# Transposes of the second token pair moved between the first products, two gate tiles for HGRN's output, and a modulation chunk moved to the last phase

## The chip, the cores and the metric

The kernel runs on one core of one Trainium2 chip. The metric is the device time of one execution in microseconds (us); several runs are summarised by their median. The profile is of one such execution.

## The reference, cut to what matters

The reference is a two-layer backbone on 512 latent tokens (and 256 context tokens) of width 1024. Each layer is half a SwiGLU feed-forward, a token mixer, and half a feed-forward; each of these is modulated before and normalised after:

```python
def modulation(cond, w_mod, b_mod):
    m = jax.nn.silu(cond) @ w_mod + b_mod          # 9 rows of 1024 a layer ("chunks")
def modulate(x, m, k):
    return x * (1 + m[..., 3 * k + 1, :]) + m[..., 3 * k, :]
def post_norm_update(x, y, m, k, g, b):
    return layer_norm(DN_ALPHA * x + m[..., 3 * k + 2, :] * y, g, b)
...
    for i in range(DEPTH):
        x = macaron_half_ffn(x, mx, 0, ffn_w_in[i, 0], ffn_w_out[i, 0], ln_g[i, 0], ln_b[i, 0])
        ...                                         # mixer: HGRN2 in layer 0, chunk-MLP in layer 1
        x = post_norm_update(x, yx, mx, 1, ln_g[i, 1], ln_b[i, 1])
        x = macaron_half_ffn(x, mx, 2, ffn_w_in[i, 1], ffn_w_out[i, 1], ln_g[i, 2], ln_b[i, 2])
```

All is float32.

## The kernel before

**Products.** Each float32 operand is split into a high and a low part: ACT copies the high part (L135), DVE subtracts it to get the low part (L136), and three matmuls (L148, L149, L150) make one product. The tiles `w` (weights), `xm` (the modulated input), `hs` (hidden units) and `f` (sums of blocks of `xm`) hold such pairs. SP loads the raw weights (`raw`, `rawu`).

**Phases.** The program is a row of output phases (class `OutPhase`, method `run`), each followed by the first products of the next block (classes `FeedIn`, `FeedSums`, `GateIn` and the like, called `nxt`). An output phase multiplies the hidden units by the second weight matrix for four tiles of 128 tokens (`nt`; two in a context phase) and two halves of 512 output columns. `lead` does this pair by pair of hidden blocks. When a half is done, `evac` multiplies each tile's sum `y` by the gate row (`rgate`, L356) and adds the residual (L358), with statistics behind (L361); after the second half `norm` finishes them (L366, two steps on POOL, L380).

**Hand-over.** Then `operand(p, kb)` makes the next input for a pair `p` of token tiles and a pair `kb` of feature blocks: four transposes on PE into `pt` (L390), the modulation by scale and shift (L400 on ACT, L402 on DVE), and the split into `xm`. There are eight such steps, o0 to o3 for tiles 0 and 1, o4 to o7 for tiles 2 and 3. `nxt.staged(p, kb)` multiplies the same piece by the first four weight units (24 matmuls for a feed-forward phase: s0 to s7). In the phases called f2 (after HGRN's output), f3 (after the first layer's last feed-forward), gin (before the chunk-MLP) and f4 (after the chunk-MLP's output) the flag `hold` is set, and two pairs of the output product of the last tile are held back and done between the steps.

**Sums.** FeedSums multiplies 2 by 2 blocks with seven products (`seven`) instead of eight: f2, f3 and f4 first add blocks of the input (`sums`, L601), and the first `seven` (`early`) interleaves these sums with its weight sums. The products are `psc`, `pse`, `psa`, `psb`; the staged ones are `psf`.

**Modulation rows.** The rows of `modulation` are computed on DVE beside other work: `scraps(pool, layer, chunks)` queues them and `mod_step(n)` does n steps for each pair of `lead`; one step loads 512 KB of the modulation weights and does two multiply-and-sum rows on DVE (L170). Chunk 8 of layer 1 is the gate of the very last feed-forward.

**Order.** Each engine has its own in-order queue. A scheduler (the tile framework) places the instructions of each engine; the order written in `run` and the number of buffers of a tile (`bufs`) decide what it can place where.

Of the kernel before, what the change touches and what calls it, by code (L numbers as in the profile page):

```python
# [28 lines left out]
NH = 8  # L29
# [41 lines left out]
def backbone_kernel(  # L71
# [148 lines left out]
    def scraps(sp, l, chs, small=None):  # L220

        if small is None:
            s, small = (sp.tile([P, D], F32, tag="e", name="e", bufs=2) for _ in range(2))
        else:
            s, small = small[:, :D], small[:, D:]
        nc.sync.dma_start(s, cond[CI_OF["x"]].partition_broadcast(P))
        nc.scalar.activation(s, s, AF.Silu)
        small = Scraps(sp, small, "rawu")
        for ch in chs:
            queue_mod(small, {"x": s}, l, ch, ["x"])  # L230

    def queue_mod(modp, srow, l, ch, conds):
        mod_queue.append(mod_task(modp, srow, l, ch, conds))
# [3 lines left out]
    def mod_step(n, after=None):  # L237

        credit[0] += n
        while credit[0] >= 1 and mod_queue:  # L240
            try:
                with tc.issue_after((after or latest[0]).ins):
                    next(mod_queue[0])
                credit[0] -= 1
            except StopIteration:
                mod_queue.pop(0)
        if not mod_queue:
            credit[0] = 0.0

    def made(key):  # L250
        d = gate_row if key[1] % 3 == 2 else mod_col
        while key not in d:
            mod_step(1 - credit[0])
        return d[key]
# [15 lines left out]
    def load_row(pool, tag, src, n=HC, bufs=1):  # L270
        r = pool.tile([P, n], F32, tag=tag, name=tag, bufs=bufs)
        nc.sync.dma_start(r, src.partition_broadcast(P))
        return r

    class OutPhase:
# [49 lines left out]

        def load_gate(self, hf):
            c = slice(hf * HC, (hf + 1) * HC)
            self.gate = load_row(self.bp, "rgate", made((self.l, 3 * self.j + 2, self.cond))[0, c])

        def store(self):  # L330

# [50 lines left out]
        def operand(self, p, kb):  # L382

            o, ks = slice(p * 2 * P, (p + 1) * 2 * P), slice(2 * kb, 2 * kb + 2)
            cols, xm = self.cols, self.xm
            pt = bank("pt").rearrange("p (k t) -> p k t", t=2 * P)
            for i in range(2):
                k = 2 * kb + i
                for t in range(2):
                    nc.tensor.transpose(  # L390
                        pt[:, i, t * P : (t + 1) * P], self.xs[2 * p + t][:, k * P : (k + 1) * P], ident
                    )
            xf = self.nxt.block(p, kb)
            if xf is None:
                xf = pt
            for i in range(2):
                k = 2 * kb + i
                g, b = cols[:, 0, k : k + 1], cols[:, 1, k : k + 1]
                if i or p or kb:
                    nc.scalar.activation(xf[:, i, :], pt[:, i, :], AF.Identity, scale=g, bias=b)  # L400
                else:
                    nc.vector.tensor_scalar(xf[:, i, :], pt[:, i, :], g, b, ALU.mult, ALU.add)  # L402
            return split(xm[:, 0, ks, o], xm[:, 1, ks, o], xf)

        def run(self, bp, hook=None, nmod=0):
            self.bp, nt, nxt = bp, self.nt, self.nxt
            self.xs, self.st = [], []
            self.load_gate(0)
            for t in range(nt):
                xt = bp.tile([P, D], F32, tag="x", name="x", bufs=NT)  # L410
                nc.sync.dma_start(xt, self.xsrc(t))
                self.xs.append(xt)
                self.st.append(bp.tile([P, 2, 6], F32, tag="st", name="st", bufs=NT))
            if self.affine:
                self.lead(0, 3, nmod)
                self.finish()
            self.lead(0, self.npair, nmod)
            for t in range(nt):
                self.evac(0, t)
            if hook:  # L420
                hook()
            self.load_gate(1)
            self.lead(1, self.npair - self.tail, nmod)
            held = [(kk, *self.operands(1, kk)) for kk in range(self.npair - self.tail, self.npair)]
            if nxt is None:
                self.last = [load_row(wpool, "raw", src[self.l, self.j], D, 3) for src in (ln_g, ln_b)]
            else:
                self.cols = operand_cols(self.l, self.j, *self.after, self.cond)
                nxt.load()

            back = 2 if nxt is not None and nxt.hold else 0
            rest = [(1, *h, [nt - 1]) for h in held[len(held) - back :]]
            for t in range(nt):
                for h in held[: len(held) - back * (t == nt - 1)]:
                    self.part(1, *h, [t])

            def done(p):
                for t in (2 * p, 2 * p + 1):
                    self.evac(1, t)
                    self.norm(t)  # L440

            def close():
                self.held.close()
                if self.release:
                    self.release()

            if nxt is None:
                close()
                done(0)
                done(1)  # L450
                return
            nxt.ahead(0)
            done(0)
            steps = [(p, kb) for p in range(nt // 2) for kb in range(KD // 2)]
            for i in range(len(steps) + 3):
                if i == back:
                    for r in rest:
                        self.part(*r)
                    close()
                    nxt.enter()  # L460
                    if nt > 2:
                        done(1)
                if i:
                    nxt.ahead(i)

                if back and i == 4:
                    nxt.staged(*steps[1])
                    nxt.staged(*steps[2])
                if i < len(steps):
                    self.operand(*steps[i])  # L470
                j = i - 2 if back and i > 3 else i - 3
                if 0 <= j < len(steps) and not (back and i == 4):
                    nxt.staged(*steps[j])
            nxt.sums()
            if self.xdst is not None:
                if nxt.whole:
                    nxt.later = self.store()
                else:
                    for t, z in enumerate(self.xs):
                        nc.sync.dma_start(self.xdst(t), z)  # L480
# [546 lines left out]
    with sbuf(name="hgo", bufs=1) as hgo, ExitStack() as late:  # L1027
# [4 lines left out]
        with sbuf(name="hg", bufs=1) as hg:  # L1032
# [226 lines left out]
            def gated(h, on, g):  # L1259
# [8 lines left out]
            op = OutPhase(  # L1268
                lambda k: hts[k], NH, lambda hf, kk: hg_w_out[hf, kk], NT, 0, 1, "x", 1.0,
                lambda t: x1[t], True, (0, 2), None, lambda t: x2[t], f2, tail=3,  # L1270
            )
            prev, done, last = None, None, None
            for h in range(NH + 1):
# [27 lines left out]
                if prev:  # L1301
                    on = outputs(h - 1, prev)
                    g, last = proj_silu(h - 1, 3, "g")
                    done = (h - 1, on, g)
# [13 lines left out]
    with sbuf(name="sp2", bufs=1) as sp, sbuf(name="hp2", bufs=1) as hp, bpools() as bp:  # L1318
# [6 lines left out]
        op = OutPhase(  # L1325
            hget, NF, ffn_units(0, 1), NT, 0, 2, "x", 0.5, lambda t: x2[t], True, (1, 0),
            xm, lambda t: x3[t], f3, tail=3,
        )
# [7 lines left out]
        op = OutPhase(  # L1336
            hget, NF, ffn_units(1, 0), NT, 1, 0, "x", 0.5, lambda t: x3[t], True, (1, 1),
            xm, lambda t: x4[t], gin, tail=3,
        )
# [5 lines left out]
    with ExitStack() as vhp_stack:  # L1345
# [3 lines left out]
        op = OutPhase(  # L1349
            lambda k: hs[k // 3][:, k % 3, :], CI // P, lambda hf, kk: cm_w_out[hf, kk], NT, 1, 1, "x", 1.0,  # L1350
            lambda t: x4[t], True, (1, 2), None, lambda t: x5[t], f4, tail=3,
        )
        op.affine = (1, 0)
        with sbuf(name="cm", bufs=1) as cm, ExitStack() as late:
# [30 lines left out]
            cu, sp = (late.enter_context(sbuf(name=n, bufs=1)) for n in ("cu", "csp"))  # L1385
# [60 lines left out]
            for j in range(0, 3 * NG, 2):  # L1446
# [8 lines left out]
                if j == 3 * NG - 2:  # L1455
                    gin.place.close()
                    mods = ExitStack()
                    modp = mods.enter_context(swap("modp4"))
# [6 lines left out]
        f4.xm = op.xm = xm  # L1465
        bp, bw = (vhp_stack.enter_context(x) for x in (bpools(), sbuf(name="bw4", bufs=1)))
        small = vhp.tile([P, NT, GC], F32, tag="vh", name="vt").rearrange("p t c -> p (t c)")
        scraps(modp, 1, (7, 6, 8), small)
        op.run(bp, None, 1.5)

    with sbuf(name="sp4", bufs=1) as sp, sbuf(name="hp4", bufs=1) as hp, bpools() as bp:
        hget = f4.rest(hp, sp)
        op = OutPhase(
            hget, NF, ffn_units(1, 1), NT, 1, 2, "x", 0.5, lambda t: x5[t], True, None,
            None, lambda t: out[t], None, tail=4,
        )
        op.affine = (1, 1)
        op.run(bp)

# [75 lines left out]
```

## Time and profile before

| what | value |
|---|---|
| runs | 2481.15, 2485.2, 2486.4 us; median 2485.2 |
| profiled execution | 2486.62 us, span 2484.9 us |
| granted TensorE clock, mean | 0.994 |
| PE busy | 2428.3 us (98%), 14907 matmuls |
| DVE busy | 1944.7 us (78%) |
| ACT busy | 1166.0 us (47%) |
| moved by DMA | 365.49 MB, mean 147 GB/s |

The span is the profiled time from the first to the last instruction; the device time includes a little around it. PE is nearly always busy, so its idle stretches and the stretches in which its clock was lowered are what can be shortened. The places that the change touches, in microseconds from the start of the span: HGRN's output ends and f2 begins at 960 to 1060; f3 at 1318 to 1420; gin at 1690 to 1800; the chunk-MLP's output at 2012 to 2120 and f4 to 2200; the last output phase at 2320 to the end.

### The profile page before, as it was taken

The numbers are of one execution on the slowest core, as the hardware profiler recorded it, in microseconds if no ns is written. First come the engines' busy times: TensorE is split into PE (matmuls) and PEld (weight loads), VectorE is DVE, ScalarE is ACT, GpSimd is POOL, SyncE is SP. The second block draws the span as 40 slices with busy tenths as digits, with TensorE's granted clock in tenths as the row PEclk, the third lists the DMA queues.
The fourth block names the chain that finished last, engine by engine and source line by source line (L and its number), as shares of the span: only waits on it lengthen the run. The fifth ranks groups of instructions, "written<-read, shape, count | busy, mean of one in ns | idle before, by whom it ended". The sixth has DMA issues, their size and how long they took to land.

```text
span 2484.9 us, 38142 instructions
## 1 busy us (share of the span) xinstructions
PE 2428.3 (98%) x14907; PEld 2194.3 (88%) x14907; DVE 1944.7 (78%) x3466; ACT 1166.0 (47%) x1821; POOL 43.4 (2%) x83
## 2 busy tenths in 40 slices
PE   7999999999999999999999999999999999899998
PEld 5888889987888888999988899889999987899986
DVE  7965678685588886788895988897898687788775
ACT  4222345454445452555543555544654442555641
POOL 0000000000000000000000000000000000000001
PEclk9999999999999999999999999999999999999999
DMA  8866556783211214333473233574323376333332
GB/s 317 294 204 199 174 187 219 261 252 125 68 60 52 60 60 154 101 116 102 153 247 126 87 110 110 177 238 139 98 100 102 111 248 201 119 116 103 102 117 74
DMA packets 106853, 365.49 MB, mean 147 GB/s; under 512 B 12408, under 2 KB 13616, under 8 KB 106672
## 3 DMA queue, kind: packets, MB, share of 16 engines
q1 hardware_dynamic: 106672, 363.06, 44.3%
q8 instruction: 116, 1.90, 0.3%
q14 instruction: 65, 0.53, 0.1%
HBM read 350.40 MB, written 12.61 MB: 146 GB/s over the span
## 4 chain that ended last, share of the span: by engine, by line
PE 78%; DVE 13%; ACT 3%; DMA 3%; issue 2%; POOL 1%; SPq 0%; POOLq 0%; DVEq 0%; ACTq 0%
PE y L150 7%; PE y L149 7%; PE y L148 7%; PE psf L150 6%; PE psf L149 6%; PE psf L148 6%; PE psc L148 5%; PE psc L150 5%; PE psc L149 5%; PE pse L148 3%; PE pse L150 3%; PE pse L149 3%; DVE w L136 2%; PE psa L149 1%; PE psa L148 1%
## 5 line engine op out<-in xcount | busy, mean ns | idle before, releaser
L136 DVE TENSOR_TENSOR w<-raw,w 128x1024 fp32r<-128x1024 f32 (+2 forms) x446 | 501.0, 1127 | 156.4 <-ACT w L135 155.4
L135 ACT ACTIVATE w<-raw 128x1024 fp32r<-128x1024 f32 (+2 forms) x446 | 436.4, 982 | 388.5 <-PE y L150 89.8
L150 PE MATMUL y<-w,hs 128*128 128x512 f32 x984 | 385.2, 392 | 8.2 <-DVE hs L136 8.2
L148 PE MATMUL y<-w,hs 128*128 128x512 f32 x984 | 385.1, 391 | 0.1
L149 PE MATMUL y<-w,hs 128*128 128x512 f32 x984 | 384.1, 390 | 0.0
L150 PEld LDWEIGHTS y<-w,hs 128*128 128x128 f32 x984 | 185.4, 189 | 49.3 <-DVE hs L136 10.9
L135 ACT ACTIVATE hs<-h 128x512 fp32r<-128x512 f32 (+1 forms) x220 | 125.9, 588 | 201.6 <-PE y L150 186.8
L148 PEld LDWEIGHTS y<-w,hs 128*128 128x128 f32 x984 | 185.3, 188 | 39.3 <-ACT hs L135 0.8
L149 PEld LDWEIGHTS y<-w,hs 128*128 128x128 f32 x984 | 185.5, 189 | 38.3
L148 PE MATMUL psf<-xm,w 128*128 128x512 f32 (+1 forms) x544 | 192.8, 358 | 13.0 <-ACT xm L135 12.8
L150 PE MATMUL psf<-xm,w 128*128 128x512 f32 (+1 forms) x544 | 192.3, 354 | 2.4 <-DVE w L136 2.4
L149 PE MATMUL psf<-xm,w 128*128 128x512 f32 (+1 forms) x544 | 192.6, 354 | 1.5 <-DVE xm L136 1.5
L136 DVE TENSOR_TENSOR hs<-h,hs 128x512 fp32r<-128x512 f32 (+1 forms) x220 | 135.2, 634 | 73.3 <-ACT hs L135 73.1
L148 PE MATMUL pse<-f,w 128*128 128x256 f32 x544 | 155.8, 286 | 5.0 <-ACT w L135 4.1
L148 PE MATMUL psc<-f,w 128*128 128x256 f32 x544 | 156.0, 287 | 4.6 <-ACT w L135 3.8
L150 PE MATMUL pse<-f,w 128*128 128x256 f32 x544 | 155.4, 286 | 0.0
L150 PE MATMUL psc<-f,w 128*128 128x256 f32 x544 | 155.4, 286 | 0.0
L149 PE MATMUL pse<-f,w 128*128 128x256 f32 x544 | 155.2, 285 | 0.0
L149 PE MATMUL psc<-f,w 128*128 128x256 f32 x544 | 154.9, 285 | 0.0
L150 PE MATMUL psc<-xm,w 128*128 128x256 f32 x532 | 151.3, 284 | 2.8 <-DVE w L136 2.8
L148 PE MATMUL psc<-xm,w 128*128 128x256 f32 x532 | 152.1, 286 | 1.8 <-ACT w L135 1.2
L149 PE MATMUL psc<-xm,w 128*128 128x256 f32 x532 | 151.0, 284 | 0.0
(343 smaller groups left out, 6028.7 us busy)
## 6 DMA issues: line engine op xcount, KB each, us to landing
raw<-in_ffn_w_in SPq DMA_DIRECT2D x160, 512.0 KB, 4.5
raw<-in_ffn_w_out SPq DMA_DIRECT2D x110, 512.0 KB, 4.2
mraw<-in_mod_w SPq DMA_DIRECT2D x80, 512.0 KB, 4.5
rawu<-in_mod_w SPq DMA_DIRECT2D x64, 512.0 KB, 4.4
rawu<-in_ffn_w_in SPq DMA_DIRECT2D x60, 512.0 KB, 3.6
x<-x SPq DMA_DIRECT2D x36, 512.0 KB, 3.6
raw<-in_hg_wf SPq DMA_DIRECT2D x32, 512.0 KB, 3.5
raw<-in_cm_w_out SPq DMA_DIRECT2D x24, 512.0 KB, 4.6
```

Of the source, the lines that this page charges most:

```text
L135: nc.scalar.activation(dst_hi, src, AF.Copy)
L136: latest[0] = nc.vector.tensor_tensor(dst_lo, src, dst_hi.bitcast(F32), ALU.subtract)
L148: nc.tensor.matmul(ps, ah, bh, start=start, stop=False, **kw)
L149: nc.tensor.matmul(ps, ah, bl, start=False, stop=False, **kw)
L150: return nc.tensor.matmul(ps, al, bh, start=False, stop=stop, **kw)
```

## The change

Four edits: `run` has a new order for phases with `hold` (written out as a list of o and s), `operand` gives the modulation of the first of its two feature blocks to DVE in every step, `load_gate(0)` comes before the last two pairs of the first half with two gate tiles in HGRN's output alone, and chunk 8 is queued in the last phase instead of the chunk-MLP's output.

```diff
--- before.py
+++ after.py
@@ -325,7 +325,8 @@
 
         def load_gate(self, hf):
             c = slice(hf * HC, (hf + 1) * HC)
-            self.gate = load_row(self.bp, "rgate", made((self.l, 3 * self.j + 2, self.cond))[0, c])
+            row = made((self.l, 3 * self.j + 2, self.cond))[0, c]
+            self.gate = load_row(self.bp, "rgate", row, bufs=2 if self.nk == NH else 1)
 
         def store(self):
 
@@ -396,7 +397,7 @@
             for i in range(2):
                 k = 2 * kb + i
                 g, b = cols[:, 0, k : k + 1], cols[:, 1, k : k + 1]
-                if i or p or kb:
+                if i:
                     nc.scalar.activation(xf[:, i, :], pt[:, i, :], AF.Identity, scale=g, bias=b)
                 else:
                     nc.vector.tensor_scalar(xf[:, i, :], pt[:, i, :], g, b, ALU.mult, ALU.add)
@@ -405,7 +406,6 @@
         def run(self, bp, hook=None, nmod=0):
             self.bp, nt, nxt = bp, self.nt, self.nxt
             self.xs, self.st = [], []
-            self.load_gate(0)
             for t in range(nt):
                 xt = bp.tile([P, D], F32, tag="x", name="x", bufs=NT)
                 nc.sync.dma_start(xt, self.xsrc(t))
@@ -414,6 +414,8 @@
             if self.affine:
                 self.lead(0, 3, nmod)
                 self.finish()
+            self.lead(0, self.npair - 2, nmod)
+            self.load_gate(0)
             self.lead(0, self.npair, nmod)
             for t in range(nt):
                 self.evac(0, t)
@@ -452,25 +454,29 @@
             nxt.ahead(0)
             done(0)
             steps = [(p, kb) for p in range(nt // 2) for kb in range(KD // 2)]
-            for i in range(len(steps) + 3):
-                if i == back:
-                    for r in rest:
-                        self.part(*r)
-                    close()
-                    nxt.enter()
-                    if nt > 2:
+            if not nxt.hold:
+                close()
+                nxt.enter()
+                for i in range(len(steps) + 3):
+                    if i == 1 and nt > 2:
                         done(1)
-                if i:
-                    nxt.ahead(i)
-
-                if back and i == 4:
-                    nxt.staged(*steps[1])
-                    nxt.staged(*steps[2])
-                if i < len(steps):
+                    if i:
+                        nxt.ahead(i)
+                    if i < len(steps):
+                        self.operand(*steps[i])
+                    if i >= 3:
+                        nxt.staged(*steps[i - 3])
+            else:
+
+                for i in range(2):
                     self.operand(*steps[i])
-                j = i - 2 if back and i > 3 else i - 3
-                if 0 <= j < len(steps) and not (back and i == 4):
-                    nxt.staged(*steps[j])
+                for r in rest:
+                    self.part(*r)
+                close()
+                nxt.enter()
+                done(1)
+                for kind, i in ("o2", "o3", "s0", "s1", "o4", "o5", "s2", "o6", "o7", "s3", "s4", "s5", "s6", "s7"):
+                    (self.operand if kind == "o" else nxt.staged)(*steps[int(i)])
             nxt.sums()
             if self.xdst is not None:
                 if nxt.whole:
@@ -1465,8 +1471,8 @@
         f4.xm = op.xm = xm
         bp, bw = (vhp_stack.enter_context(x) for x in (bpools(), sbuf(name="bw4", bufs=1)))
         small = vhp.tile([P, NT, GC], F32, tag="vh", name="vt").rearrange("p t c -> p (t c)")
-        scraps(modp, 1, (7, 6, 8), small)
-        op.run(bp, None, 1.5)
+        scraps(modp, 1, (7, 6), small)
+        op.run(bp, None, 1)
 
     with sbuf(name="sp4", bufs=1) as sp, sbuf(name="hp4", bufs=1) as hp, bpools() as bp:
         hget = f4.rest(hp, sp)
@@ -1475,7 +1481,8 @@
             None, lambda t: out[t], None, tail=4,
         )
         op.affine = (1, 1)
-        op.run(bp)
+        scraps(sp, 1, (8,))
+        op.run(bp, None, 1)
```

Lines of the changed kernel are shifted: L356 is L357 there, L402 is L403, L601 is L607, L661 is L667.

DVE's queue at f3's hand-over before, from the last tile's second-half evacuation (`st` are its statistics, `mv` mean and variance) to the first sums (L601):

```order
1378 L361 BN_STATS st<-x 128x6
1379 L136 TENSOR_TENSOR xm<-h,xm 128x2x256
1380 L366 BN_AGGR mv<-st 128x2
1381 L136 TENSOR_TENSOR xm<-h,xm 128x2x256
1382 L380 TENSOR_SCALAR x<-x,mv,rstd 128x1024
1383 L136 TENSOR_TENSOR xm<-h,xm 128x2x256 x4
1384 L136 TENSOR_TENSOR w<-raw,w 128x1024
1385 L601 TENSOR_TENSOR h<-h 128x512 x4
1386 L680 TENSOR_TENSOR e<-raw,rawu 128x512
1387 L136 TENSOR_TENSOR f_12769<-h,f_12769 128x512 x2
```

The same place in the changed kernel; L403 is the modulation:

```order
1387 L362 BN_STATS st<-x 128x6
1388 L403 TENSOR_SCALAR h<-pt,opc 128x256
1389 L367 BN_AGGR mv<-st 128x2
1390 L136 TENSOR_TENSOR xm<-h,xm 128x2x256
1391 L381 TENSOR_SCALAR x<-x,mv,rstd 128x1024
1392 L136 TENSOR_TENSOR xm<-h,xm 128x2x256
1393 L403 TENSOR_SCALAR h<-pt,opc 128x256 x2
1394 L136 TENSOR_TENSOR xm<-h,xm 128x2x256 x2
1395 L403 TENSOR_SCALAR h<-pt,opc 128x256 x2
1396 L136 TENSOR_TENSOR xm<-h,xm 128x2x256 x2
1397 L136 TENSOR_TENSOR w<-raw,w 128x1024
1398 L607 TENSOR_TENSOR h<-h 128x512 x4
```

Before, the second pair's modulations were all on ACT and have no row here; now each of its steps has one modulation on DVE, ahead of its `xm` split. On PE the transposes of o4 and o5 stood behind s0, s1 and s2, and those of o6 and o7 behind s3 and s4; now o4 and o5 stand behind s1, and o6 and o7 behind s2.

SP's queue at the end of HGRN's output before: loads of the gate rows (`rgate`), the residual (`x`), the next weights and the affine rows (`rg`, `rb`):

```order
202 L141 DMA raw<-in_ffn_w_in 128x1024 x4
203 L272 DMA rgate<-gr_5_x 128x512
204 L411 DMA x<-x_83 128x1024 x4
205 L661 DMA raw<-in_ffn_w_in 128x1024
206 L272 DMA rgate<-gr_8_x 128x512
207 L272 DMA rg<-in_ln_g 128x512
208 L661 DMA raw<-in_ffn_w_in 128x1024
209 L272 DMA rgate<-gr_5_x 128x512
210 L272 DMA rb<-in_ln_b 128x512
```

The same place in the changed kernel:

```order
200 L141 DMA raw<-in_ffn_w_in 128x1024 x4
201 L411 DMA x<-x_83 128x1024 x4
202 L272 DMA rgate<-gr_5_x 128x512 x2
203 L667 DMA raw<-in_ffn_w_in 128x1024 x2
204 L669 DMA rawu<-in_ffn_w_in 128x1024
205 L486 DMA x_84<-x 128x1024
206 L669 DMA rawu<-in_ffn_w_in 128x1024
```

Both halves of the gate row are loaded together, behind the four x loads; the next phase's gate row and the affine rows have gone from between them to later rows.

DVE's queue in the chunk-MLP's output before, from within the evacuation of the third tile's first half to the next split of hidden units (`hs`); `vt` is the modulation's scratch:

```order
2182 L358 TENSOR_TENSOR x<-x,t_19822 128x512
2183 L170 SCALAR_TENSOR_TENSOR vt<-rawu,vt 128x512
2184 L361 BN_STATS st<-x 128x6
2185 L356 SCALAR_TENSOR_TENSOR t_19826<-y_19265,rgate 128x512
2186 L170 SCALAR_TENSOR_TENSOR vt<-rawu,vt 128x512
2187 L358 TENSOR_TENSOR x<-x,t_19826 128x512
2188 L170 SCALAR_TENSOR_TENSOR vt<-rawu,vt 128x512
2189 L361 BN_STATS st<-x 128x6
2190 L183 TENSOR_REDUCE vt<-vt 128x8
2191 L170 SCALAR_TENSOR_TENSOR vt<-rawu,vt 128x512
2192 L194 SCALAR_TENSOR_TENSOR mc_6_x<-vt,mbT 128x8
2193 L136 TENSOR_TENSOR hs<-ht,hs 128x512
```

The changed kernel, from the evacuation of the second tile on:

```order
2194 L136 TENSOR_TENSOR w<-raw,w 128x1024
2195 L362 BN_STATS st<-x 128x6
2196 L357 SCALAR_TENSOR_TENSOR t_19798<-y_19263,rgate 128x512
2197 L136 TENSOR_TENSOR hs<-ht,hs 128x512
2198 L359 TENSOR_TENSOR x<-x,t_19798 128x512
2199 L136 TENSOR_TENSOR hs<-ht,hs 128x512
2200 L362 BN_STATS st<-x 128x6
2201 L357 SCALAR_TENSOR_TENSOR t_19802<-y_19264,rgate 128x512
2202 L170 SCALAR_TENSOR_TENSOR vt<-rawu,vt 128x512
2203 L359 TENSOR_TENSOR x<-x,t_19802 128x512
2204 L170 SCALAR_TENSOR_TENSOR vt<-rawu,vt 128x512
2205 L362 BN_STATS st<-x 128x6
```

The next `hs` splits stand two tiles earlier, and there are fewer modulation rows between the evacuations.

## Prediction

> **What bounds the kernel.** I read the page first, then the windows stage by stage, then the timelines of PE and DVE where PE stands. The page:
>
> ```profile
> PE 2428.3 (98%) x14907; PEld 2194.3 (88%) x14907; DVE 1944.7 (78%) x3466; ACT 1166.0 (47%) x1821; POOL 43.4 (2%) x83
> PE 78%; DVE 13%; ACT 3%; DMA 3%; issue 2%; POOL 1%; SPq 0%; POOLq 0%; DVEq 0%; ACTq 0%
> ```
>
> PE is the bound: it idles 2484.9 − 2428.3 = 56.6 us in all, and DVE carries 13% of the chain of waits. The change removes no matmul, so it can only win idle time of PE, and time at a lowered clock. The windows say where that lies (length, then busy us of PE, PEld, DVE, ACT, POOL, then PEclk, the granted clock, and the DMA share):
>
> ```profile
> 960.00:1010.00 50.00, 46.37 (x290) 41.44 (x289) 29.00 (x45) 16.01 (x27) 3.78 (x8) 1.00 0.62 216
> 1010.00:1060.00 50.00, 47.71 (x369) 46.02 (x368) 48.01 (x73) 31.56 (x54) 0.00 (x0) 0.97 0.26 85
> 1318.00:1372.00 54.00, 53.53 (x352) 48.94 (x351) 31.03 (x48) 22.01 (x39) 3.49 (x8) 1.00 0.36 123
> 1372.00:1420.00 48.00, 42.16 (x320) 40.97 (x319) 43.77 (x66) 26.68 (x46) 0.00 (x0) 0.93 0.32 99
> 1690.00:1800.00 110.00, 109.61 (x624) 106.19 (x623) 93.79 (x136) 65.28 (x109) 3.48 (x8) 1.00 0.35 119
> 2012.00:2070.00 58.00, 51.40 (x214) 41.63 (x213) 53.84 (x120) 18.76 (x26) 0.00 (x0) 0.94 0.70 222
> 2147.00:2200.00 53.00, 47.10 (x360) 45.91 (x359) 48.27 (x71) 29.55 (x50) 0.00 (x0) 0.94 0.47 154
> 1376.78:1380.19 3.41, 2.93 (x12) 2.63 (x12) 3.41 (x6) 0.59 (x2) 0.00 (x0) 0.50 0.16 23
> ```
>
> Idle plus (1 − PEclk) × length gives what each stage can win at most: end of HGRN's output 3.6; f2's first seven products 2.3 + 1.5 = 3.8; f3 0.5 + 5.8 + 3.4 = 9.7; gin 0.4; chunk-MLP output 6.6 + 3.5 = 10.1; f4 5.9 + 3.2 = 9.1. Together 36.7 us. The last row is one of the half-clock stretches: 3.41 us at 0.50, so 1.7 us lost each.
>
> **f3 (run's new order, modulation split).** PE's timeline, and DVE's behind it:
>
> ```profile
> 1353.81 1.03 PE L390 MATMUL pt<-ident,x 128*128 128x128 f32 x8
> 1357.55 0.60 PE L390 MATMUL pt<-ident,x 128*128 128x128 f32 x4
> 1360.86 0.60 PE L390 MATMUL pt<-ident,x 128*128 128x128 f32 x4
> 1376.25 0.39 PE L148 MATMUL psc<-f,w 128*128 128x256 f32 x1 [1.85 <-ACT w L135]
> 1386.21 0.39 PE L150 MATMUL psc<-xm,w 128*128 128x256 f32 x1 [1.42 <-DVE w L136]
> 1389.70 0.39 PE L148 MATMUL pse<-f,w 128*128 128x256 f32 x1 [2.04 <-ACT w L135]
> ```
>
> ```profile
> 1349.82 0.81 DVE L380 TENSOR_SCALAR x<-x,mv,rstd 128x1024 f32<-128x1024 f32 x1 [0.77 <-POOL rstd L370]
> 1356.47 0.69 DVE L136 TENSOR_TENSOR xm<-h,xm 128x512 fp32r<-128x512 f32 x1 [5.84 <-ACT xm L135]
> 1357.59 0.69 DVE L136 TENSOR_TENSOR xm<-h,xm 128x512 fp32r<-128x512 f32 x1 [0.43 <-ACT xm L135]
> 1359.90 0.69 DVE L136 TENSOR_TENSOR xm<-h,xm 128x512 fp32r<-128x512 f32 x1 [1.61 <-ACT xm L135]
> 1363.22 0.69 DVE L136 TENSOR_TENSOR xm<-h,xm 128x512 fp32r<-128x512 f32 x1 [2.63 <-ACT xm L135]
> 1364.96 1.29 DVE L601 TENSOR_TENSOR h<-h 128x512 f32<-128x512 f32 x2
> ```
>
> The waits named "w" are the end of a longer story. DVE idles 5.84 + 0.43 + 1.61 + 2.63 = 10.5 us between 1350 and 1363, because the second pair's transposes (8, 4 and 4) come between blocks of staged products; the last four stand at 1360.86. Only then can the block sums (L601) start, at 1364.96, 3.5 us after those transposes end at 1361.46; from there DVE is full and PE waits for it.
>
> In the new order o4 and o5 follow two blocks instead of three, o6 and o7 one block later. A block is 24 matmuls; that from the first of these transposes to the next is 1357.55 − 1353.81 = 3.74 us, less eight transposes (1.03, with the last one's overlap off 0.87), so 2.9. Tile 3 is normalised at 1350.6, about when the second block ends (2.9 before 1353.81), so o4 waits 0 to 0.4 us for DVE there. Then 0.9 for o4 and o5, 2.9 for a block, 0.9 for o6 and o7: transposes done about 1355.3. With the same 3.5 us behind them the sums start about 1358.8, 6.2 us earlier.
>
> What the earlier start buys: the three quoted waits and two of 0.28 and 0.26 between them make 5.85, and the first half-clock stretch holds PE back another 1.7, so DVE is about 7.5 us late at the last wait. Less 6.2 leaves 1.3. Gain 9.7 − 1.3 − 0.4 = 8.0. Ends: 9.7 if nothing remains; 3 if the start moves by half as much.
>
> The price of the split stands in these rows:
>
> ```profile
> L402 DVE TENSOR_SCALAR h<-pt,opc x2: 529/529/529, 1340.9 to 1699.9; 128x256 f32<-128x256 f32 x2
> L400 ACT ACTIVATE h<-pt,opc x30: 549/565/589, 1341.1 to 1717.8; 128x256 f32<-128x256 f32 x30
> L170 DVE SCALAR_TENSOR_TENSOR vt<-rawu,vt x48: 671/684/695, 1992.9 to 2085.8; 128x512 bf16<-128x512 f32 x48
> ```
>
> Seven modulations a phase go to DVE at 0.53 us (some 0.45 start to start), 3.2 us a phase, 38 in all or 17 us. In f2, f3 and f4 they fall into the idle 10.5 us, so they cost nothing; without that cover the 3.2 would stand ahead of the sums. ACT gets 38 × 0.565 = 21 us back, but it is 47% busy and that is worth nothing.
>
> **f4 and f2.** f4 has the same order and shape; gain by the same steps 9.1 − 1.3 = 7.8 (ends 3 and 9.1). f2 has idle of the same size before its sums and loses 3.8 behind them, less than the sums gain: 3.6 (ends 1.5 and 3.8).
>
> **gin.** Its blocks hold half as many matmuls, so two of them cover less of the normalisation of tile 3 than in f3; the idle there, 0.4, may go and a new wait may come. I take 0 (ends −0.4, and +1.5, twice the 0.77 for which the quoted normalisation waits).
>
> **HGRN's output end (two gate tiles).**
>
> ```profile
> 959.71 0.43 SPq L272 DMA_DIRECT2D rgate<-gr_x  x1
> 965.41 0.69 DVE L356 SCALAR_TENSOR_TENSOR t<-y,rgate 128x512 f32<-128x512 f32 x1 [5.50 <-DMA rgate<-gr_x]
> 978.42 0.69 DVE L356 SCALAR_TENSOR_TENSOR t<-y,rgate 128x512 f32<-128x512 f32 x1 [2.71 <-DMA rgate<-gr_x]
> 983.53 0.44 PE L390 MATMUL pt<-ident,x 128*128 128x128 f32 x2 [1.40 <-DVE x L380]
> 986.19 0.88 PE L390 MATMUL pt<-ident,x 128*128 128x128 f32 x6 [2.23 <-DVE x L380]
> 962.00:966.00 4.00, 4.00 (x19) 3.32 (x18) 0.59 (x1) 1.06 (x1) 0.00 (x0) 1.00 0.76 270
> 966.00:970.00 4.00, 4.00 (x20) 3.30 (x19) 3.90 (x7) 1.06 (x1) 0.00 (x0) 1.00 1.01 391
> ```
>
> Before, gate 0 is the first load and gate 1 waits for the tile. Now both are issued at once, but behind four x loads of 512 KB on SP's queue, 2.1 MB. Of that up to 0.8 landed before the gate anyway (4 us at 270 GB/s, less the gate's 0.26 MB); the other 1.3 at 391 GB/s put gate 0 3.2 us later, at 968.6. DVE does two weight splits (1.13 each) in that wait instead of behind it, and gate 1's 2.71 is gone, so that the second half's evacuation starts 3.2 − 2.3 − 2.7 = 1.8 us earlier, at 976.6. Gain 1.7. Ends: 3.6 (both PE waits go) and a loss of 1.5 (gate 0 two us later still, up to which 978.42 would be kept, and more beyond).
>
> **Chunk-MLP output (a chunk fewer).**
>
> ```profile
> 2043.65 0.68 DVE L356 SCALAR_TENSOR_TENSOR t<-y,rgate 128x512 f32<-128x512 f32 x1
> 2059.44 0.69 DVE L136 TENSOR_TENSOR hs<-ht,hs 128x512 fp32r<-128x512 f32 x1
> 2060.18 0.79 PE L150 MATMUL y<-w,hs 128*128 128x512 f32 x1 [5.21 <-DVE hs L136]
> ```
>
> From 2043.65 the first half's evacuation and ten modulation rows (0.61 start to start, two to a step) stand ahead of the hs split at 2059.44, for which PE waits 5.21. With one step a pair instead of 1.5 DVE's order brings the next hs split into the second tile's evacuation, with one modulation row ahead of it. That wait goes, and the half clock behind it: 5.2 + 3.5 = 8.7; I take 8.0, for 0.7 that the gate row, now ahead of a row of the affine part on SP's queue, can add to the 1.4 us that remain early in the stage. Ends 9 and 0.
>
> **Last phase (chunk 8 added).** Eight steps, that is 16 rows or 10 us of DVE, and their eight loads of 512 KB on SP's queue move here; SP also passes the gate's store and load:
>
> ```profile
> 1240.00:1310.00 70.00, 70.00 (x311) 57.96 (x310) 62.95 (x120) 29.31 (x40) 0.00 (x0) 1.00 0.70 231
> 2320.00:2410.00 90.00, 90.00 (x538) 80.63 (x538) 64.86 (x89) 47.28 (x74) 0.00 (x0) 1.00 0.37 115
> ```
>
> DVE has 25 of 90 us free there, and the first row is an output phase that carries one step a pair already, with PE full at DMA share 0.70. The gate is now made and read back in the phase that uses it; DVE may wait 3 us for it at the first evacuation, with hs splits done 3 pairs ahead. So 0 (ends 0 and +2).
>
> **The phase before the context's output.** Here the split has no cover:
>
> ```profile
> 395.00:405.00 10.00, 9.99 (x84) 9.75 (x83) 9.90 (x19) 10.00 (x20) 0.00 (x0) 1.00 0.71 233
> 397.98 1.22 DVE L136 TENSOR_TENSOR w<-raw,w 128x1024 fp32r<-128x1024 f32 x1
> 406.98 0.28 PE L148 MATMUL psf<-xmc,w 128*128 128x256 f32 x1
> ```
>
> DVE is 99% busy and gets seven modulations or 3.2 us more, and DVE's order puts the weight split of 397.98 behind all operands, some 6 us later. PE wants it at 406.9, it was there at 399.1: the margin of 7.8 shrinks to about 1.8 and holds. 0 (ends 0 and +3).
>
> **Sum:** −8.0 − 7.8 − 3.6 − 1.7 − 8.0 = −29.1 us. The profiled execution took 2486.6, 1.4 over the median of the runs shown; so 2457.5 by the profile, 2456 as a median.
>
> **The clock.** In this trace each half-clock stretch of 3.41 us follows a wait of PE of 1.2 to 5.2 us (1376.78 follows that of 1.85). [...]
>
> **Rivals.**
> - *DVE stays the bound.* The sums start 3 us earlier, not 6.2, because the new DVE rows and the weight splits line up ahead of them. For it: DVE is full from 1365 on. Against it: 10.5 us of idle. f3, f4 gain 3 to 3.5 each, f2 2: −6.5 − 2 − 1.7 − 8 = −18, 2467.
> - *The half clock stays*, because it has another cause than these waits: 3.4 + 3.2 + 1.5 + 3.5 = 11.6 of the gain is not had, 2468. The order of wait and stretch in the rows speaks against it. [...]
> - *Slower: DVE's queue, not the transposes, sets when the sums start.* Then every moved modulation stands on the path, 38 × 0.45 = 17, against 9.7 from the gate tiles and the chunk: 2485 + 7 = 2492. It decides if f3's sums start no earlier than 1364.96. The idle rows speak against it.
> - *The last phase pays for its chunk:* 5 us of waits at the first half's end as in the stage the chunk left: 2461.
> - *No change:* the waits are for weights that come late for another reason (DMA): 2485. DMA shares of 0.26 to 0.47 in those windows speak against it.
>
> **Chances.** Forecast 0.62 (own range 2450 to 2463), DVE stays the bound 0.19, half clock stays 0.05, last phase pays 0.04: faster by over 0.2% (5 us, about what a measurement tells from no change) 0.90. No change 0.04, slower 0.06. The range 2446 to 2470 takes in the full 36.7 below, and the first two rivals above.
>
> **What would show it.** Right: at f3 16 transposes done by 1356, sums near 1359, PE idle from there to 1420 under 2 us; PEclk 1.00 in that window; no 5-us wait in the chunk-MLP output; one wait for a gate at HGRN's output, near 968. Wrong: sums in f3 later than 1362, a PE wait near 407 in the context's phase, or PE waiting for hs near the last phase's first evacuation.

## The result, and the profile after

The changed kernel takes 2453.03 us (median; 2452.43 to 2453.68), the kernel before 2485.07 (2481.15 to 2486.4): a ratio of 0.9874, 95% interval 0.9857 to 0.9891. That is 32 us faster; 2456 was forecast, in a range of 2446 to 2470. The profiled execution has a span of 2452.0 us, 32.9 less than before. Its page, by which PE idles 2452.0 − 2415.9 = 36.1 us instead of 56.6:

```profile
PE 2415.9 (99%) x14907; PEld 2185.4 (89%) x14907; DVE 1959.3 (80%) x3504; ACT 1151.4 (47%) x1784; POOL 44.3 (2%) x83
```

PE busy also fell by 12.4 us, with the same 14907 matmuls: that is the half clock gone (the granted clock was 0.994 before and is 0.999 now, which over the two spans makes 14.9 and 2.5 us lost). The windows that answer to those of before, moved with the program (length; busy us of PE, PEld, DVE, ACT, POOL; granted clock, DMA share, GB/s):

```profile
960.00:1010.00 50.00, 46.38 (x289) 40.97 (x288) 37.28 (x61) 15.71 (x25) 3.78 (x8) 1.00 0.43 156
1010.00:1060.00 50.00, 49.49 (x411) 49.08 (x410) 49.01 (x74) 31.94 (x54) 0.00 (x0) 1.00 0.48 164
1310.00:1364.00 54.00, 53.88 (x344) 48.81 (x343) 39.18 (x62) 21.85 (x36) 3.45 (x8) 1.00 0.38 128
1364.00:1412.00 48.00, 47.92 (x396) 47.42 (x395) 47.01 (x69) 29.69 (x51) 0.00 (x0) 1.00 0.34 110
1676.00:1786.00 110.00, 108.55 (x620) 105.58 (x619) 96.41 (x142) 62.84 (x102) 4.40 (x8) 1.00 0.35 119
1990.00:2048.00 58.00, 57.38 (x254) 47.20 (x253) 53.80 (x110) 23.00 (x31) 0.00 (x0) 1.00 0.67 212
2123.00:2176.00 53.00, 53.00 (x441) 52.70 (x440) 51.06 (x75) 31.36 (x56) 0.00 (x0) 1.00 0.50 170
2290.00:2380.00 90.00, 90.00 (x525) 79.87 (x524) 73.78 (x125) 47.63 (x73) 0.00 (x0) 1.00 0.56 173
```

Idle plus clock deficit, before to after: end of HGRN's output 3.6 to 3.6; f2 3.8 to 0.5; f3 (two rows) 9.7 to 0.2; gin 0.4 to 1.5; chunk-MLP output 10.1 to 0.6; f4's sevens 9.1 to 0. The clock is 1.00 in all of them, and the last phase's first 90 us, with chunk 8 in them, are full. That is 30 of the 32.9 us; the other 2 us lie in small pieces elsewhere, for which no cause is shown.

f3's hand-over, PE's transposes first, then DVE's rows up to the sums:

```profile
1344.89 1.37 PE L391 MATMUL pt<-ident,x 128*128 128x128 f32 x8
1348.97 1.04 PE L391 MATMUL pt<-ident,x 128*128 128x128 f32 x8
```

```profile
1344.41 0.81 DVE L381 TENSOR_SCALAR x<-x,mv,rstd 128x1024 f32<-128x1024 f32 x1 [0.46 <-POOL rstd L371]
1348.01 1.29 DVE L136 TENSOR_TENSOR xm<-h,xm 128x512 fp32r<-128x512 f32 x2 [1.16 <-ACT xm L135]
1351.76 1.29 DVE L136 TENSOR_TENSOR xm<-h,xm 128x512 fp32r<-128x512 f32 x2 [1.16 <-ACT xm L135]
1354.11 2.49 DVE L607 TENSOR_TENSOR h<-h 128x512 f32<-128x512 f32 x4
```

The whole phase lies 5.4 us earlier here (tile 3's normalisation at 1344.41, before at 1349.82); the sums lie 10.85 us earlier (1354.11, before 1364.96). So against the phase they start 5.4 us earlier, and DVE's idle of 10.5 us between is down to the two waits of 1.16 and smaller ones. PE idles 0.08 us from 1364 to 1412.

The end of HGRN's output is the place where nothing was won. Rows of ACT, DVE and PE, and the gate loads (start, and us to landing):

```profile
967.57 1.06 ACT L135 ACTIVATE w<-raw 128x1024 fp32r<-128x1024 f32 x1 [4.38 <-PE y L150]
968.67 1.23 DVE L136 TENSOR_TENSOR w<-raw,w 128x1024 fp32r<-128x1024 f32 x1 [4.21 <-ACT w L135]
969.81 0.68 DVE L357 SCALAR_TENSOR_TENSOR t<-y,rgate 128x512 f32<-128x512 f32 x1
978.00 0.67 DVE L357 SCALAR_TENSOR_TENSOR t<-y,rgate 128x512 f32<-128x512 f32 x1
983.09 0.44 PE L391 MATMUL pt<-ident,x 128*128 128x128 f32 x2 [0.59 <-DVE x L381]
986.76 1.53 PE L391 MATMUL pt<-ident,x 128*128 128x128 f32 x12 [1.62 <-DVE x L381]
```

```profile
L272 SPq DMA_DIRECT2D rgate<-gr_x x2: 436/460/484, 960.9 to 961.4; - x2
...
DMA to landing us min/median/max: 7.6/7.7/7.7
```

The first gate lands at 968.6, but a weight split that is not ready before 968.67, because ACT's copy for it starts only at 967.57, stands ahead of the evacuation, which starts at 969.81. (The row for this could be read before: there the same copy starts at 968.56, behind the same wait of 4.38 for PE.) The second half's starts at 978.00; the program lies 1 us earlier here than before, so against it that is 0.5 us later than before's 978.42.

### The profile page after: what moved, and what is told of

Same layout as the page of the kernel before. It is cut to its first block, busy times and chain, and to the rows that moved or that the text cites. A ratio compares the mean times of both kernels' runs of the same rounds, so it can differ in the third digit from the quotient of the medians.

```text
span 2452.0 us, 38155 instructions
## 1 busy us (share of the span) xinstructions
PE 2415.9 (99%) x14907; PEld 2185.4 (89%) x14907; DVE 1959.3 (80%) x3504; ACT 1151.4 (47%) x1784; POOL 44.3 (2%) x83
## 4 chain that ended last, share of the span: by engine, by line
PE 79%; DVE 13%; ACT 3%; issue 2%; DMA 2%; POOL 1%; SPq 0%; POOLq 0%; DVEq 0%; ACTq 0%
PE y L150 8%; PE y L148 8%; PE y L149 8%; PE psf L150 5%; PE psf L149 5%; PE psf L148 5%; PE psc L148 5%; PE psc L149 5%; PE psc L150 5%; PE pse L150 2%; PE pse L148 2%; PE pse L149 2%; DVE w L136 2%; PE psa L148 1%; PE psa L150 1%
```

## The experiments

**Each edit alone.** Four kernels, each the kernel before with one edit. First the order of `run` (the list of o and s of the diff above, the rest as before):

> The kernel before with the new order of transposes and products alone; modulation, gate tiles and chunk 8 as before. Theory A (the place of the second pair's transposes sets when the sums start): f2, f3 and f4 lose nearly all of their idle time, about -21 us, 2464 us; f3's sums start some 4 to 5 us earlier against the phase than before. Theory B (the modulations on ACT set it as well, 1.1 us for each step): about half, -10 us, 2475 us, with PE waits left in f3 and f4.

Measured 2464.23 us, ratio 0.9905 (0.989 to 0.992), 22 us less than the kernel before took beside it: theory A. f3's window behind the sums, and DVE's waits for ACT that remain:

```profile
1364.00:1412.00 48.00, 47.88 (x395) 47.33 (x395) 46.77 (x70) 29.23 (x52) 0.00 (x0) 1.00 0.34 110
```

```profile
1349.89 0.69 DVE L136 TENSOR_TENSOR xm<-h,xm 128x512 fp32r<-128x512 f32 x1 [2.96 <-ACT xm L135]
1353.63 0.69 DVE L136 TENSOR_TENSOR xm<-h,xm 128x512 fp32r<-128x512 f32 x1 [1.92 <-ACT xm L135]
```

DVE still waits for ACT's modulations, 2.96 and 1.92, but PE idles 0.12 of 48 us. The sums start 4.8 us earlier against tile 3's normalisation than before. So the new order, with the second pair's transposes moved forward, was the cause.

Then the split of the modulation:

```diff
-                if i or p or kb:
+                if i:
```

> The kernel before with one of the two modulations of every step on DVE, and nothing else. Theory A: the sums start 0.5 us earlier in each of f2, f3 and f4, -1.5 us together, 2483 to 2485 us. Theory B: -10 us, 2475 us. Rival from the prediction (38 more rows on a full DVE): slower by 3 us or more, with a PE wait near 407 in the phase before the context's output.

Measured 2484.02 us, ratio 0.9992 (0.9982 to 1.0002): no difference that can be told, as theory A had it; theory B and the rival of the prediction fell. In f3 the sums start about 0.5 us earlier, and PE idles 4.27 us behind them instead of 5.84.

The gate (two tiles in HGRN's output, late `load_gate(0)`):

> The kernel before with two gate tiles in HGRN's output and the late load of the first gate, and nothing else. Theory A (the first evacuation now stands behind a weight split that comes later than the gate): no gain, -0.5 to +1 us, 2485 us, PE's idle at the end of HGRN's output stays near 3.6. Theory B (prediction's term): -1.7 us there.

Measured 2484.53 us, ratio 0.9989 (0.998 to 0.9998). In size that is theory B's gain, but not in place: HGRN's end did not change, as theory A says. What moved is in the chunk-MLP's output: its first wait (1.40 before) is gone and the second is 3.66 instead of 5.21:

```profile
2056.64 0.79 PE L150 MATMUL y<-w,hs 128*128 128x512 f32 x1 [3.66 <-DVE hs L136]
```

And there is a surprise in f2:

```profile
1010.00:1060.00 50.00, 47.70 (x381) 46.00 (x380) 48.65 (x73) 31.42 (x54) 0.00 (x0) 1.00 0.41 143
```

f2 has here the idle time of before (2.30, before 2.29), with the same longest wait, 1.2 us; but the clock is 1.00 where it was 0.97; in f3 it is 0.91 over the 20 us from 1374 to 1394, 1.8 us lost, where 0.93 over 48 us made 3.4. So part of this run's gain is the clock, and the profile gives no reason to count that to the gate.

Chunk 8:

```diff
-        scraps(modp, 1, (7, 6, 8), small)
-        op.run(bp, None, 1.5)
+        scraps(modp, 1, (7, 6), small)
+        op.run(bp, None, 1)
...
+        scraps(sp, 1, (8,))
-        op.run(bp)
+        op.run(bp, None, 1)
```

> The kernel before with chunk 8 moved to the last phase, and nothing else. Theory A: PE's wait of 5.2 us and the half clock behind it in the chunk-MLP's output go, -8 to -9 us, 2476 us, and the last phase stays without idle time. Theory B: the work costs the same in the last phase, 2481 to 2485 us, with waits of PE between 2330 and 2420.

Measured 2498.3 us, ratio 1.0043 (1.0028 to 1.0058): slower, and both theories missed. The chunk-MLP's output lost its long wait, as expected; but in the last phase PE stands for 15 us (the timeline of PE, then the window around it, then SP's queue):

```profile
2363.29 0.38 PE L187 MATMUL pg<-ident,e 128*8 128x128 f32 x1 [14.96 <-DVE e L185]
```

```profile
2350.00:2440.00 90.00, 76.71 (x329) 63.31 (x330) 62.78 (x97) 32.10 (x44) 0.00 (x0) 0.91 0.37 115
```

```profile
2349.66 6.99 SPq L176 DMA_DIRECT2D rawu<-in_mod_w  x3
...
2364.85 0.32 SPq L191 DMA_DIRECT2D gr_x<-e  x1
...
2367.93 0.33 SPq L272 DMA_DIRECT2D rgate<-gr_x  x1
```

`load_gate(0)` stood at the phase's start, and it asks for the gate row (`made`), which runs whatever of its chunk is still queued. So all eight steps come in a row, and the row's transpose (`pg`), which PE has in its queue there, holds up the products behind it. This is read from the trace; the next two runs test it.

**Gate and chunk together.** That reading says that the late load, which looked like a detail of HGRN's output, is what makes room for chunk 8:

> The kernel before with chunk 8 in the last phase and the late load of the first gate (and HGRN's two gate tiles); order and modulation as before. Theory A (with the early load, asking for the gate row at the phase's start makes all of chunk 8's steps run there at once, ahead of PE's first transpose of the row; the late load lets them spread): the 15-us wait at the last phase's start is gone, the chunk-MLP's output loses about 10 us of idle time and half clock, 2474 to 2477 us. Theory B (chunk 8 costs its 15 us in the last phase whatever the gate's place): 2490 us or more.

Measured 2475.85 us, ratio 0.9958 (0.9943 to 0.9973), 11 us less than before: theory A. The chunk-MLP's output and the last phase, both full:

```profile
2005.00:2063.00 58.00, 58.00 (x257) 48.03 (x257) 54.13 (x112) 22.87 (x32) 0.00 (x0) 1.00 0.67 214
2320.00:2430.00 110.00, 110.00 (x586) 95.22 (x585) 87.66 (x142) 54.87 (x81) 0.00 (x0) 1.00 0.49 157
```

That kernel differs from the one with the chunk alone by all late loads and by HGRN's tiles. So the load of the last phase alone was put back to its start in the changed kernel:

```diff
+            if self.nxt is None:
+                self.load_gate(0)
...
-            self.load_gate(0)
+            if self.nxt is not None:
+                self.load_gate(0)
```

> The changed kernel with the load of the first gate at the start of the last phase again, and late in all others. Theory A (asking for the gate row there forces all of chunk 8 at once, as in the run with chunk 8 alone): a PE wait of about 15 us near 2310 with half clock behind it, 15 + 3 to 5 us, 2471 to 2474 us. Theory B (the late loads of the other phases are what saved the run of gate and chunk): 2453 to 2456 us.

Measured 2469.99 us, ratio 0.9941 (0.9924 to 0.9957), 17 us over the changed kernel. The wait is back, at the row's transpose:

```profile
2336.74 0.38 PE L187 MATMUL pg<-ident,e 128*8 128x128 f32 x1 [15.43 <-DVE e L185]
```

Theory A: 15.43 of the 17 us are the wait, so some 1.6 are left for half clock, less than the 3 to 5 expected. The granted clock is 0.60 from 2320 to 2340, most of it within the wait:

```profile
2320.00:2340.00 20.00, 4.57 (x20) 3.69 (x20) 18.45 (x43) 5.94 (x10) 0.00 (x0) 0.60 0.54 176
```

**The split in the changed kernel.** The first condition put back (`if i or p or kb`):

> The changed kernel with the modulations on ACT again, all but the first. Theory A (the order is enough; the split only starts the sums some 2 us earlier, and PE does not wait for them any more): 2452 to 2455 us, no PE wait over 1 us in f3 and f4. Theory B (the split is needed): 2457 us or more, with waits in f2, f3 and f4.

Measured 2455.45 us, ratio 0.9876 (0.9861 to 0.9891; the changed kernel's was 0.9874), span 2453.1. f3's window up to the sums shows 0.49 idle instead of 0.12; behind them nothing changed:

```profile
1310.00:1364.00 54.00, 53.51 (x338) 48.37 (x338) 34.63 (x53) 24.07 (x41) 3.48 (x8) 1.00 0.38 131
1364.00:1412.00 48.00, 47.90 (x396) 47.35 (x395) 46.94 (x70) 29.44 (x52) 0.00 (x0) 1.00 0.34 110
```

The split is worth 1 to 2 us by the medians and spans, and by the ratios it can't be told from nothing; the time is just past the top of theory A. No long wait came back: the split is not what PE waited for. The reverse, both modulations of every step on DVE (`if i > 1`), asks how much room DVE has:

> The changed kernel with both modulations of every step on DVE (another 40 rows of 0.45 us from start to start). Theory A (f2, f3 and f4 have cover; the phase before the context's output has a margin of some 1.5 us left at the weight split wanted at 407): no wait back in f3 and f4, PE waits of 1 to 4 us in all between 400 and 425, 2454 to 2458 us. Theory B (no stage is close to DVE): 2453 us. Theory C (DVE bounds the first sevens too): 2460 us or more with waits in f2, f3 and f4.

Measured 2461.52 us, ratio 0.9904 (0.9889 to 0.9919). f2, f3 and f4 have no wait, as theory A says, and the context's phase has one of 1.12 at 405. But most of the loss, and the time past theory A's 2458, is in a stage that no theory named, gin:

```profile
405.00 0.39 PE L150 MATMUL psf<-xmc,w 128*128 128x256 f32 x1 [1.12 <-DVE w L136]
1716.38 0.50 PE L149 MATMUL pscv<-w,xm 128*128 128x384 f32 x1 [4.59 <-DVE w L136]
```

**HGRN's gates.** One tile again (`bufs=1`), the late load kept:

> The changed kernel with one gate tile in HGRN's output too (the late load stays). Theory A (late first gate and second gate in a row): the second gate is asked for after the first half's evacuation, near 977, lands 4 us later, the second half starts near 981 instead of 978.0, PE's idle at the end of HGRN's output 3.6 + 3, 2456 us. Theory B (the second half's start does not set PE's wait): 2453 us.

Measured 2458.48 us, ratio 0.989 (0.9874 to 0.9907). The second gate's wait and its effect on PE, and the window:

```profile
981.17 0.69 DVE L357 SCALAR_TENSOR_TENSOR t<-y,rgate 128x512 f32<-128x512 f32 x1 [3.50 <-DMA rgate<-gr_x]
```

```profile
987.10 1.11 PE L391 MATMUL pt<-ident,x 128*128 128x128 f32 x4 [3.67 <-DVE x L381]
```

```profile
960.00:1010.00 50.00, 43.20 (x250) 37.63 (x249) 33.42 (x54) 12.81 (x20) 4.96 (x8) 0.93 0.59 211
```

Theory A for the wait (981.17, 6.8 us idle); the other 2 us or more over its 2456 are half clock (0.93 over the 50 us, 3.5 us lost). So with one tile the late load would cost HGRN's output some 5 us, and the second tile gives them back: the two cancel. That suggests both gates ahead of the x loads:

```diff
+            early = [self.load_gate(0), self.load_gate(1)] if self.nk == NH else None
...
-            self.load_gate(0)
+            self.gate = early[0] if early else self.load_gate(0)
```

(`load_gate` returns the tile here, and the second half takes `early[1]` likewise.)

> The changed kernel with both gate rows of HGRN's output loaded ahead of the four x loads. Theory A (the gate's place behind the x loads and the weight split ahead of the evacuation ate the gain of the second tile): first evacuation near 965, the second half's near 975.5 instead of 978.0, PE's idle at the end of HGRN's output from 3.6 to about 1, 2450 to 2451 us. Theory B (the second half's evacuation is bound by the normalisations on DVE, not by its start): 2453 us.

Measured 2451.08 us (2450.34 to 2451.36), ratio 0.9858 (0.9844 to 0.9873): theory A in mechanism. By the medians that is 2 us less than the changed kernel; the two ratios' intervals overlap, but all four runs of the changed kernel lie above these, and so do all four of the next run, measured beside these. The evacuation waits for the gate again, but at 964, and the second half's follows without one:

```profile
964.09 0.69 DVE L357 SCALAR_TENSOR_TENSOR t<-y,rgate 128x512 f32<-128x512 f32 x1 [5.18 <-DMA rgate<-gr_x]
974.50 0.67 DVE L357 SCALAR_TENSOR_TENSOR t<-y,rgate 128x512 f32<-128x512 f32 x1
```

```profile
958.00:1008.00 50.00, 48.12 (x299) 42.91 (x299) 38.87 (x63) 15.82 (x25) 3.75 (x8) 1.00 0.45 158
```

PE's idle here is 1.9 instead of 3.6, which is where the 2 us come from; 1.9 is a little more than expected.

**gin's order.** In gin alone o4 and o5 behind three products:

```diff
+                late = ("s2", "o4", "o5", "s3", "o6", "o7") if isinstance(nxt, GateIn) else ("o4", "o5", "s2", "o6", "o7", "s3")
+                for kind, i in ("o2", "o3", "s0", "s1", *late, "s4", "s5", "s6", "s7"):
```

> The changed kernel, in gin alone with the transposes of o4 and o5 behind three products (o2 o3 s0 s1 s2 o4 o5 s3 o6 o7 s4 ...). Theory A (gin's shorter products don't cover the normalisation of tile 3): the wait of 1.3 us at 1695 goes, 2452 us. Theory B: the sums start later and the wait comes back behind them, 2453 us or more.

Measured 2453.32 us: no gain. The wait for tile 3's normalisation is 0.89 instead of 1.11, and smaller ones stand beside it. It is DVE's chain of normalisations that PE waits for, and one product more does not cover it:

```profile
1695.71 0.77 PE L391 MATMUL pt<-ident,x 128*128 128x128 f32 x5 [0.89 <-DVE x L381]
```

## Why the prediction was right, and where not

- **f3, f4 and f2** (−8.0, −7.8, −3.6): right in mechanism, shown by the order alone (0.9905). Measured −9.5, about −9.5 with the half microsecond ahead of f4's sums, and −3.3. The forecast of the start was nearly right: the second pair's transposes end 4.8 us after tile 3 is normalised (4.7 forecast), and the sums follow 4.1 us behind them instead of 3.5. The step that was mis-sized is "so DVE is about 7.5 us late at the last wait. Less 6.2 leaves 1.3.": the sums came only 5.4 us earlier, and still no wait was left. Before, DVE was not full through those waits:

```profile
1381.90 0.42 DVE L746 TENSOR_TENSOR h<-pse,sc 128x256 f32<-128x256 f32 x1 [0.95 <-PE pse L150]
1380.00:1390.00 10.00, 6.32 (x48) 5.92 (x49) 8.92 (x17) 4.65 (x9) 0.00 (x0) 0.99 0.35 102
```

  It idled 1.1 of 10 us there, 0.95 of it waiting for PE, so part of its lateness was that of PE coming back to it. Adding up PE's waits counts that part twice. The run with the split alone fits this, 0.5 us of earlier sums for 1.57 us less idle, but its clock in f3 differs too (1.00 from 1372 to 1383 and 0.81 from 1383 to 1392, 1.7 us lost, where 0.93 over 48 us made 3.4); so this is the likely reason, not a shown one.
- **HGRN's end** (−1.7): wrong, 0. The step that failed is that DVE would do both weight splits while it waits for the gate: the second was not ready before 968.67, so it stood behind the gate's landing and ahead of the evacuation, some 1.2 us. The gate landed at the forecast 968.6, but that is partly luck: the program lies 1 us earlier here, so against it the gate came some 4 us later than before, not 3.2. The run with the gates first and the one with one tile show that the gates' place and number do set this stage.
- **Chunk-MLP's output** (−8.0): −9.5. The wait at the third tile went as forecast. The early wait of 1.4, which was to stay or grow by 0.7, shrank to 0.62; with the gate edit alone it is gone.
- **Last phase** (0): right as a sum, but for a reason that the prediction did not state. It allowed DVE a wait of 3 us for the gate, a size that no run shows; DVE waits 0.33. SP's store and load of the row, and DVE's first evacuation:

```profile
2372.57 0.29 SPq L191 DMA_DIRECT2D gr_x<-e  x1
...
2374.94 0.42 SPq L272 DMA_DIRECT2D rgate<-gr_x  x1
```

```profile
2378.96 0.69 DVE L357 SCALAR_TENSOR_TENSOR t<-y,rgate 128x512 f32<-128x512 f32 x1 [0.33 <-DMA rgate<-gr_x]
```

  That chunk 8 is spread at all rests on the late load; without it the last phase pays a wait of 15.43 us and half clock (0.60 from 2320 to 2340), 17 us in all. The prediction priced the two edits apart and named no tie between them.
- **gin** (0, up to +1.5): +1.1, inside its bounds; its own new wait for the normalisation.
- **The context's phase** (0, margin 1.8): right. The weight split wanted at 406.9 starts here at 404.20 or behind that with a second one, so the first is done near 405.4 and both by 406.55, and PE waits for neither. With forty more rows on DVE PE waits 1.12 there.

```profile
404.20 2.35 DVE L136 TENSOR_TENSOR w<-raw,w 128x1024 fp32r<-128x1024 f32 x2
```

- **The half clock** went with the waits, and the rival that it stays fell: the granted clock is 1.00 in all eight windows of the changed kernel above, and was 0.93 to 0.97 in f2, f3, the chunk-MLP's output and f4 before. But a wait was not always followed by a stretch: PE idles 2.29 us in f2 in the kernel before and 2.31 with the chunk alone, with the clock at 0.97 in both, and 2.30 with the gate alone, at 1.00 (last section). And the stretch at the wait of 5.21 does not only follow it: it is 6.83 us long and starts at 2059.44, before that wait ends at 2060.18. That stretch in the kernel before, and f2 with the chunk alone:

```profile
2059.44:2066.27 6.83, 6.09 (x14) 4.79 (x15) 6.68 (x17) 0.00 (x0) 0.00 (x0) 0.50 0.66 193
1010.00:1062.00 52.00, 49.69 (x385) 48.01 (x385) 49.63 (x75) 32.06 (x55) 0.00 (x0) 0.97 0.25 82
```

## What to carry to other kernels

Where PE waits for a full engine, look for that engine's idle time before the wait: here 10.5 us of DVE's lay ahead of f3's waits, and the new order, which moves the sixteen transposes of the second pair forward in each such phase, was worth two thirds of the gain. A call that asks for a result also decides when the work behind it runs; spread work must be asked for after its last step. Edits tied in this way don't add: alone the order, the split, the gate and the chunk came to −22, −2, −2 and +12 us, together to −32. Gate and chunk taken as one came to −11, and with the order's −22 that does add up.

## What the runs showed of the hardware

The same four waits of PE in f2 (0.36, 0.36, 1.18 and 0.36 us in the kernel before, 0.37, 0.36, 1.19 and 0.36 with the gate alone) were followed by 3.41 us at half clock in the kernel before, and by none in the run with the gate alone (1.00 in its window above). In the kernel before, the longest wait:

```profile
1027.25 0.39 PE L148 MATMUL psc<-xm,w 128*128 128x256 f32 x1 [1.18 <-ACT w L135]
```

The 3.41 us ahead of the stretch, and the stretch:

```profile
1025.21:1028.62 3.41, 1.87 (x14) 1.46 (x13) 3.34 (x6) 2.72 (x5) 0.00 (x0) 1.00 0.18 71
1028.62:1032.03 3.41, 3.41 (x18) 3.41 (x18) 3.27 (x7) 1.77 (x3) 0.00 (x0) 0.50 0.53 154
```

In this trace the half-clock stretches of f2 and f3 start at 1028.62, 1376.78 and 1390.43: 102 and 4 times 3.413 us apart, a step worked out from these starts. Those at 2059.44, 2151.60 and 2165.26 follow 196, 27 and 4 such steps later, each after the one before it. In the 3.41 us ahead of the first three, PE was busy for 1.87, 1.54 and 1.37:

```profile
1373.37:1376.78 3.41, 1.54 (x11) 1.13 (x9) 3.41 (x7) 2.68 (x5) 0.00 (x0) 1.00 0.00 0
1387.02:1390.43 3.41, 1.37 (x12) 1.17 (x11) 3.41 (x6) 2.22 (x3) 0.00 (x0) 1.00 0.00 0
```

But as little busy time was followed by no stretch elsewhere. With the gate alone the 3.41 us at the same place against the longest wait, 1026.98 to 1030.39, have PE busy for 1.86, added up from the rows of its timeline, and the clock stays at 1.00:

```profile
1029.02 0.39 PE L148 MATMUL psc<-xm,w 128*128 128x256 f32 x1 [1.19 <-ACT w L135]
1026.00:1034.00 8.00, 6.46 (x52) 6.04 (x51) 7.93 (x14) 5.72 (x10) 0.00 (x0) 1.00 0.88 344
```

With the order alone PE idles twice in the chunk-MLP's output, for 2.55 us from 2002 to 2006 and for 2.35 from 2045 to 2048. Half clock follows the first, 1.7 us lost from 2005 to 2012, and none the second:

```profile
2002.00:2006.00 4.00, 1.45 (x7) 0.88 (x5) 3.90 (x8) 1.77 (x3) 0.00 (x0) 0.94 0.06 23
2005.00:2012.00 7.00, 6.13 (x21) 4.98 (x22) 7.00 (x17) 0.73 (x2) 0.00 (x0) 0.76 0.51 151
2045.00:2048.00 3.00, 0.65 (x3) 0.19 (x1) 3.00 (x10) 1.13 (x2) 0.00 (x0) 1.00 0.74 251
2047.00:2056.00 9.00, 7.95 (x34) 6.42 (x35) 8.93 (x23) 1.27 (x2) 0.00 (x0) 1.00 0.62 190
```

What decides it is not shown.

So a wait of 1.2 us was followed by a loss of 1.7 us more in one run and by none in another, and comparing two kernels by the time of one such stage can mislead by that much.
